# Gate block 1 in seven-product steps, its weight sums begun earlier, in a float32 residual block on one core

## The chip, the cores and the metric

One core of one Trainium2 chip runs the whole program. A core has TensorE (matrix products into the eight PSUM banks), VectorE, ScalarE and GpSimd (elementwise work) and queues that issue DMAs; SP, ScalarE and GpSimd issue them here. The profile calls the engines PE (PEld for its weight loads), DVE, ACT, POOL and SP. The metric is device time in microseconds, a median over runs.

## The reference

One layer of a residual block on x of 512 positions by 1024 channels, all in float32 (cut to what matters):

```python
h = rms_norm(x, norm_mix_g)
cb, cc, cin, q, k, v, f_logit, g_logit = jnp.split(h @ w_in, ...)
u = causal_dwconv(cc * cin, conv_mix_w)
y_conv = (cb * u) @ w_out_conv
o = forgetting_attention(q, k, v, log_sigmoid(f_logit + b_f))   # 8 heads of 64
y_attn = o @ w_out_attn
g_conv, g_attn = jnp.split(sigmoid(g_logit + b_gate), 2, axis=-1)   # 2 x 1024 channels
x = x + (g_conv * y_conv + g_attn * y_attn) @ w_o
a, b = jnp.split(causal_dwconv(rms_norm(x, norm_ffn_g) @ w_up, conv_ffn_w), 2, axis=-1)
x = x + (silu(a) * b) @ w_down
return rms_norm(x, norm_f_g)
```

## The kernel before

Activations lie transposed, channels on the 128 partitions and the 512 positions along the free dimension; 1024 channels are KB = 8 blocks. Every float32 operand is used as a high and a low part (`wh`, `wl` of a weight, `xgh`, `xgl` of the normalised input), and a product is three matmuls: high by high, low weight by high x, high weight by low x. One such matmul has 128 weights columns and 256 positions.

Weights stream in chunks in the order of the list `stream`. A chunk is loaded by an SP DMA into a ring of buffers (`load`; the ring `raw` holds four chunks), then split: ScalarE copies the rounded high part (`wh_...`, L275) and VectorE subtracts (`wl_...`, L279). High and low parts have two buffers each, so a split waits until TensorE is done with the chunk before the last.

The stages follow each other on TensorE: values (`pa`, `pb`); queries and keys of two head pairs (`q0`, `k0`, `q1`, `k1`, functions `proj` and `evac_qk`); the attention, 37 steps in which scores, transposes and weighted values alternate with the halves of the other projections; then a loop over the eight output blocks j that makes the gates, the two branch outputs (`mix` chunk, banks `yc` and `ya`), and the merged block; then `w_o`, the up projection and the down projection in two phases.

In the gate loop a block can be made in two ways. Plain: two `proj` calls, 2 x 8 x 3 x 2 = 96 matmuls. Or in seven-product steps (`seven`, `gate_pair`): the 2 x 2 blocks of weights and of x are combined in sums, so that seven products replace eight, 84 matmuls for a block. Such a step (a pair of quarters q of the 1024 inputs) reads two chunks: P, plain weight blocks, from the input, and F, sums of weight blocks. The sums are made in DRAM by DMAs ahead of time (`make_forms`): for a group of two steps six DMAs, three copies issued on SP and three accumulating ones (`add`) issued on GpSimd's queue, each of which needs the one before to have landed. `slot()` marks a place in the program; a DMA set for slot s is issued when the count reaches s. GROUPS gives for each kind of step the steps per group, the slots between the six DMAs, and the slots between groups. Sums of x are made once: `x_scale` and `x_sums` in the attention, then `x_split(q)` cuts quarter q into `xth` (ScalarE) and `xtl` (VectorE). Small deferred pieces like these wait in the list `later`; `run_later` issues them with splits that have room, `flush` all that is left, `flush_only` those with a given tag.

Blocks j < GJ are plain; block 0 is made at the end of the attention (chunks `in20`, `in28`, in `gp`). A merged block needs the gates times rb1 (VectorE, L891), a sigmoid (ScalarE, with a load of its table), the products with `yc` and `ya` (VectorE, L987, L988), their sum on GpSimd (L989), and its parts `mh` (ScalarE) and `ml` (VectorE). The order of DMAs and matmuls is that of the program; a scheduler sets the order of the rest on each engine.

Of the kernel before, what the change touches and what calls it, by code (L numbers as in the profile page):

```python
# [16 lines left out]
KB = D // P  # L17
# [34 lines left out]
    + (((1, 6),), ((1, 7), (1, 8)), ((1, 9), (1, 10))),  # L52
)

GJ = 2
GATES = tuple(((j, q), (j, q + 1)) for j in range(GJ, KB) for q in (0, 2))

PLAIN = [(m, k) for m in (6, 7) for k in range(*PHASES[1])]
# [5 lines left out]
DOUBLES = GATES + UPD[0] + STEPS[0] + UPD[1] + STEPS[1]  # L64
NU = [len(GATES), len(GATES + UPD[0] + STEPS[0])]
ND = [NU[i] + len(UPD[i]) for i in range(2)]
GROUPS = {"gate": (2, 4, 1), "up0": (2, 4, 1), "up1": (2, 4, 1), 0: (2, (0, 3, 14, 18, 22, 26), 1), 1: (2, 3, 1)}


@with_exitstack  # L70
def block_kernel(ctx, tc, xT, vecs, wv, win, wmix, wo, wup, wst, wdp, outT):
# [3 lines left out]
    nc = tc.nc  # L75
# [6 lines left out]
    def keep(ins):  # L82
        return tc.keep_in_program_order(ins)
# [4 lines left out]
    def ring(*ids):  # L88
        st = [0]

        def f(name):
            st[0] += 1
            return bank(ids[(st[0] - 1) % len(ids)], name)

        return f
# [45 lines left out]
    ff0 = len(stream)  # L141
# [22 lines left out]
        return st  # L164

    def tag_of(k):
        return "raw" if stream[k][0][0] != "F" else "rf" if k >= ff0 else "rg"

    def load(upto):
        for k in range(len(raws), min(upto, len(stream) - 1) + 1):  # L170
            nm, src, ncol = stream[k]
            tag = tag_of(k)
            if held[tag] == NRAW[tag] or tag not in pools:
                return
            held[tag] += 1
            raw = pools[tag].tile([P, D], F32, tag=tag, name=f"raw_{nm}", bufs=NRAW[tag])
            if k == 0:

                keep(nc.scalar.dma_start(raw[:, VB:ncol], src[:, VB:]))
                keep(nc.sync.dma_start(raw[:, :VB], src[:, :VB]))  # L180
            else:
                keep(nc.sync.dma_start(raw[:, :ncol], src if tag == "raw" else made[src]))
            raws.append(raw[:, :ncol])


# [2 lines left out]
    made, todo_bg = {}, []  # L188

    def make_forms(n0, n1, key, start=0):  # L190

        size, step, shift = GROUPS[key]
        if not start:
            make_forms.slot = 0
        cuts = [n0]
        for n in range(n0 + 1, n1 + 1):
            if n == n1 or n - cuts[-1] == size or len(DOUBLES[n]) != len(DOUBLES[cuts[-1]]):
                cuts.append(n)
        for g, (a, b) in enumerate(zip(cuts, cuts[1:])):
            m = len(DOUBLES[a]) * P  # L200
            f = dr.tile([P, b - a, 4 * m], F32, tag=f"f{a}", name=f"f{a}")
            w = wst[a:b].rearrange("n p c -> p n c")
            x0, x1, x2 = w[:, :, 3 * m : 5 * m], w[:, :, 5 * m : 7 * m], w[:, :, 7 * m : 8 * m]
            for n in range(a, b):
                made[n] = f[:, n - a, :]

            def put(dst, src):
                return lambda: keep(nc.sync.dma_start(dst, src))

            def add(dst, src):  # L210
                return lambda: keep(nc.gpsimd.dma_start(dst, src, accum_op=ALU.add))  # L211

            f0, f1, f2 = f[:, :, : 2 * m], f[:, :, 2 * m : 3 * m], f[:, :, 3 * m :]
            ops = (put(f0, x0), add(f0, x1), put(f1, f[:, :, :m]), add(f1, x1[:, :, m:]), put(f2, f1), add(f2, x2))
            todo_bg.extend((start + (step * k if isinstance(step, int) else step[k]) + shift * g, op) for k, op in enumerate(ops))
        todo_bg.sort(key=lambda w: w[0])

    def slot():

# [33 lines left out]
    def split(hl=None):  # L253

        k = len(parts)
        if k == len(stream):
            return
        nm, _, ncol = stream[k]
        load(k + (LOOK if len(raws) > KB else AHEAD))
        if hl is None:  # L260
            hl = []
            for x in "hl":
                if k == 0:
                    wp.tile([P, PADW[x]], F32, tag=f"pad{x}", name=f"pad_{x}")
                w0 = VOFF if k < KB else 0
                hl.append(wp.tile([P, D], F32R, tag=f"w{x}", name=f"w{x}_{nm}", bufs=2)[:, w0 : w0 + ncol])
        hi, lo = hl
        raw = raws[k]
        if k == 0:
            for cs in (slice(VB, S + H), slice(0, VB)):  # L270
                keep(nc.vector.tensor_copy(hi[:, cs], raw[:, cs]))
        elif k == 1:
            keep(nc.vector.tensor_copy(hi, raw))
        else:
            ins = nc.scalar.activation(hi, raw, AF.Copy)  # L275
            order["hi"] = ins.ins
            if k < KB:
                keep(ins)
        ins = nc.vector.tensor_sub(lo, raw, hi.bitcast(F32))  # L279
        order["lo"] = ins.ins  # L280
        if k < KB:
            keep(ins)
        held[tag_of(k)] -= 1
        parts.append((hi, lo))
        if any(("e",) in w[2] for w in later):
            run_later(k, {"u": 4.2, "P": 1.6, "F": 1.2}[nm[0]])
            return
        run_later(k, {"u": 1.7, "P": 1.6, "F": 0.75, "i": 3.0, "m": 3.0, "d": 0 if nm == "dp1" else 2.1}.get(nm[0], 3.5))
# [80 lines left out]
    def rstd_sb(pb, name):  # L369
        rb = cp.tile([P, S], F32, tag="rb", name=f"rb_{name}")  # L370
        nc.scalar.activation(rb, pb, AF.Copy)
        return rb
# [130 lines left out]
    def proj(idx, name, evac, bank):  # L503
        st = {}

        def half(i):
            if i == 0:
                st["w"] = chunk(f"in{idx}")
                st["p"] = bank(f"p_{name}")
            wh, wl = st["w"]  # L510
            for kb in range(4 * i, 4 * i + 4):
                ks = slice(kb * P, (kb + 1) * P)
                mm3(st["p"], wh[:, ks], wl[:, ks], xgh[:, kb, :], xgl[:, kb, :], kb == 0, kb == KB - 1)
            if i == 1:

                while len(parts) < chunk.n + 2:
                    split()
                with after_split():
                    evac(st["p"])

        return [lambda: half(0), lambda: half(1)]
# [151 lines left out]
    def run_all(fs):  # L673
        for f in fs:
            f()

    split()
    split()

# [45 lines left out]
    for t in (2, 3):  # L725
        evac_v(1, t)

    st = []
    f0, f1 = proj(12, "q0", st.append, ring(7))
    f0()  # L730
    rb1 = rstd_sb(rstd_bc(rc1, NT, 6, "n1"), "n1")
    f1()
    pz = bank(4, "pz")
# [3 lines left out]
        ))  # L737
    with after_split():
        forget()
    run_all(proj(16, "k0", st.append, ring(6)))  # L740
    with after_split():
        forget_rows()
        evac_qk(0, True)(st[0])
        evac_qk(0, False)(st[1])
    run_all(proj(13, "q1", evac_qk(1, True), ring(0)))
    run_all(proj(17, "k1", evac_qk(1, False), ring(1)))
    acc, bank_s, bank_t = ring(2, 0, 1), ring(3, 4), ring(5, 6)

    for q in range(4):
# [41 lines left out]
    units = [(pr, e, qb) for pr in range(4) for hf in range(2) for qb in (2 * hf, 2 * hf + 1) for e in range(2)]  # L791
    LT, LA = 3, 5
    n = len(units)
    make_forms(0, len(GATES), "gate")
    for i in range(n + LA):
        slot()
        if i < n:
# [6 lines left out]
        if 0 <= i - LA < n:  # L804
            pr, e, qb = units[i - LA]
            if e == 1 and qb % 2 == 1:
                attend(pr, qb // 2)
    assert not todo_bg
    at.close()

    halves_of = "p (h c) -> p h c"
# [6 lines left out]
    def split_next():  # L818
        if len(parts) == chunk.n and stream[chunk.n][0] not in ("dp1", "dp2"):
            split()  # L820
# [60 lines left out]

    def mt(name):
        mt.n += 1
        return xm[:, (mt.n + 3) % KB, :]

    mt.n = 0

    def evac_gate(idx, dst):
        def f(p):
# [69 lines left out]
    for j in range(KB):  # L959
        gs = []  # L960
        for _ in range(3):
            slot()
        if j == KB - 1:
            assert mt.n == 3 * KB
            x1 = xm
            nc.gpsimd.dma_start(x1[:, :4, :], xT[:, :4, :])
        if j == 0:
            evac_gate(0, gs)(gp[0])
            evac_gate(8, gs)(gp[1])
        elif j < GJ:  # L970
            run_all(proj(20 + j, f"ga{j}", evac_gate(j, gs), acc))
            run_all(proj(28 + j, f"gb{j}", evac_gate(8 + j, gs), acc))
        else:
            if j == GJ:
                acc = ring(3, 4, 2, 7)
            seven(GATES[2 * (j - GJ) : 2 * (j - GJ) + 2], 2 * (j - GJ), {j: (0, 1, 5, 6)}, gate_form, done=gate_pair(j, gs))
        wh, wl = chunk(f"mix{j}")
        yc, ya = acc(f"yc{j}"), acc(f"ya{j}")
        for pp, hh, ll, o in ((yc, ych, ycl, 0), (ya, oth, otl, 4)):
            for k in range(4):  # L980
                ks = slice((o + k) * P, (o + k + 1) * P)
                mm3(pp, wh[:, ks], wl[:, ks], hh[:, k, :], ll[:, k, :], k == 0, k == 3)
        if j >= GJ:
            split_next()
            flush()
        a, b = gs
        nc.vector.tensor_mul(a, a, yc)  # L987
        nc.vector.tensor_mul(b, b, ya)  # L988
        nc.gpsimd.tensor_add(a, a, b)  # L989
        nc.scalar.activation(mh[:, j, :], a, AF.Copy)  # L990
        nc.vector.tensor_sub(ml[:, j, :], a, mh.bitcast(F32)[:, j, :])
# [550 lines left out]
```

## Time and profile before

| what | us |
|---|---|
| median of 3 runs (lowest to highest) | 691.93 (691.58 to 691.97) |
| profiled execution: span, the only time the page gives for it | 690.3 |
| TensorE busy | 682.4 |
| VectorE busy | 556.0 |
| ScalarE busy | 368.5 |
| GpSimd busy | 190.9 |

The span runs from the first to the last instruction of one profiled execution. A timeline row gives the start, the time taken, the engine, the line, the operation, what is written and read, the shapes, how many instructions are merged, and in brackets the idle time of the engine before it and what ended it. The attention ends at about 182 us in this profile, block 0's `mix` matmuls begin at 182.60, block 1's gates at 188.11, and block 2's at 204.43.

### The profile page before, as it was taken

How to read it: one execution, taken by the hardware profiler on the slowest of the kernel's cores; microseconds unless marked ns; L12 is line 12 of the kernel's file. 1: busy time of each engine (PE TensorE's matmuls, PEld its weight loads, DVE VectorE, ACT ScalarE, POOL GpSimd, SP SyncE). 2: the span in 40 equal slices, each digit the busy share in tenths (PEclk: the TensorE clock that was granted, in tenths of full speed). 3: DMA queues.
4: the chain of work that ended last, by engine and by line, in shares of the span. 5: the costliest groups of instructions: out<-in, count | busy, mean ns of one | idle time of the engine just before them, and what ended most of it. 6: DMA issues, size and time to landing. Idle time of an engine off the chain costs nothing.

```text
span 690.3 us, 14714 instructions
## 1 busy us (share of the span) xinstructions
PE 682.4 (99%) x5936; PEld 681.1 (99%) x5936; DVE 556.0 (81%) x861; ACT 368.5 (53%) x581; POOL 190.9 (28%) x203
## 2 busy tenths in 40 slices
PE   9999999999999999999999999999999999999996
PEld 9999999999999999999999999999999999999995
DVE  6677887966578778868879699998786998998894
ACT  5575755555555444446554455546444555445672
POOL 6124946543021201213410144330100314332000
PEclk9999999999999999999999999999999999999998
DMA  8628999562577586788997498889945996776613
GB/s 309 221 62 287 216 239 219 124 138 88 166 168 204 165 263 203 231 311 213 162 309 232 126 241 233 179 240 257 248 150 172 296 265 166 172 186 167 186 31 123
DMA packets 66165, 137.54 MB, mean 199 GB/s; under 512 B 5888, under 2 KB 31760, under 8 KB 65840
## 3 DMA queue, kind: packets, MB, share of 16 engines
q1 hardware_dynamic: 45384, 107.28, 47.0%
q0 software_dynamic: 18896, 26.03, 24.4%
q10 hardware_dynamic: 1816, 3.29, 1.3%
q8 instruction: 46, 0.75, 0.4%
q14 instruction: 23, 0.19, 0.1%
HBM read 132.31 MB, written 47.71 MB: 261 GB/s over the span
## 4 chain that ended last, share of the span: by engine, by line
PE 99%; DVE 0%; DVEq 0%; issue 0%
PE dn L327 29%; PE p_up L309 21%; PE p_in L309 14%; PE p_up L327 6%; PE p_wo L309 6%; PE yc L309 3%; PE ya L309 3%; PE pa L477 2%; PE pb L479 2%; PE p_q L309 2%; PE p_k L309 2%; PE o L658 2%; PE tp L641 1%; PE pdB L309 1%; PE pdA L309 1%; PE s L612 1%
## 5 line engine op out<-in xcount | busy, mean ns | idle before, releaser
L211 POOL DMA_DIRECT2D f<-in_wst_dram x69 | 79.6, 1350 | 26.7 <-DMA f<-f 26.4
L309 PE MATMUL p_up<-x1h,wh_up 128*128 128x256 f32 x416 | 81.1, 276 | 0.0
L309 PE MATMUL p_up<-x1l,wh_up 128*128 128x256 f32 x416 | 81.0, 276 | 0.0
L309 PE MATMUL p_up<-x1h,wl_up 128*128 128x256 f32 x416 | 80.9, 276 | 0.0
L279 DVE TENSOR_TENSOR wl_F<-raw_F,wh_F 128x1024 fp32r<-128x1024 f32 (+1 forms) x43 | 56.1, 1304 | 19.0 <-ACT wh_F L275 18.9
L275 ACT ACTIVATE wh_F<-raw_F 128x1024 fp32r<-128x1024 f32 (+1 forms) x43 | 44.5, 1034 | 39.9 <-PE dn L327 26.4
L309 PEld LDWEIGHTS p_up<-x1h,wh_up 128*128 128x128 f32 x416 | 62.7, 188 | 0.0
L309 PEld LDWEIGHTS p_up<-x1l,wh_up 128*128 128x128 f32 x416 | 62.6, 188 | 0.0
L309 PEld LDWEIGHTS p_up<-x1h,wl_up 128*128 128x128 f32 x416 | 62.6, 188 | 0.0
L309 PE MATMUL p_in<-xgh,wh_in 128*128 128x256 f32 x288 | 56.8, 279 | 0.0
L309 PE MATMUL p_in<-xgh,wl_in 128*128 128x256 f32 x288 | 56.6, 278 | 0.0
L309 PE MATMUL p_in<-xgl,wh_in 128*128 128x256 f32 x288 | 56.5, 278 | 0.0
L1235 POOL TENSOR_TENSOR ge<-fu,fu 128x512 f32<-128x512 f32 x11 | 21.6, 1968 | 124.1 <-DVE fu L570 94.0
L279 DVE TENSOR_TENSOR wl_P<-raw_P,wh_P 128x768 fp32r<-128x768 f32 (+1 forms) x43 | 42.2, 981 | 14.5 <-ACT wh_P L275 8.7
L275 ACT ACTIVATE wh_P<-raw_P 128x768 fp32r<-128x768 f32 (+1 forms) x43 | 35.3, 820 | 33.5 <-PE dn L327 23.1
L327 PE MATMUL dn<-gl,wh_F 128*128 128x256 f32 x216 | 51.0, 276 | 0.0
L327 PE MATMUL dn<-gh,wh_F 128*128 128x256 f32 x216 | 51.0, 276 | 0.0
L279 DVE TENSOR_TENSOR wl_up<-raw_up,wh_up 128x1024 fp32r<-128x1024 f32 x34 | 45.2, 1328 | 6.3 <-ACT wh_up L275 6.3
L275 ACT ACTIVATE wh_up<-raw_up 128x1024 fp32r<-128x1024 f32 x34 | 35.9, 1055 | 20.7 <-PE p_up L309 10.1
L309 PEld LDWEIGHTS p_in<-xgh,wh_in 128*128 128x128 f32 x288 | 44.7, 188 | 0.7
L309 PEld LDWEIGHTS p_in<-xgl,wh_in 128*128 128x128 f32 x288 | 43.7, 188 | 0.0
L309 PEld LDWEIGHTS p_in<-xgh,wl_in 128*128 128x128 f32 x288 | 43.6, 188 | 0.0
(343 smaller groups left out, 2212.1 us busy)
## 6 DMA issues: line engine op xcount, KB each, us to landing
raw_F<-f SPq DMA_DIRECT2D x40, 512.0 KB, 5.5
raw_up<-in_wup_dram SPq DMA_DIRECT2D x34, 512.0 KB, 5.5
raw_P<-in_wst_dram SPq DMA_DIRECT2D x40, 384.0 KB, 5.7
raw_in<-in_win_dram SPq DMA_DIRECT2D x24, 512.0 KB, 3.8
f<-in_wst_dram POOLq DMA_DIRECT2D x41, 256.0 KB, 7.4
f<-in_wst_dram SPq DMA_DIRECT2D x19, 512.0 KB, 7.2
f<-in_wst_dram POOLq DMA_DIRECT2D x19, 512.0 KB, 8.4
f<-f SPq DMA_DIRECT2D x38, 256.0 KB, 6.0
```

What stands on the lines that cost most here:

```text
L211: return lambda: keep(nc.gpsimd.dma_start(dst, src, accum_op=ALU.add))
L275: ins = nc.scalar.activation(hi, raw, AF.Copy)
L279: ins = nc.vector.tensor_sub(lo, raw, hi.bitcast(F32))
L309: keep(nc.tensor.matmul(out[:, cs], w, x[:, cs], start=start and i == 0 and c == 0, stop=stop and i == 2 and c == len(cut) - 1,))
L327: keep(nc.tensor.matmul(out, wl if x == 1 else wh, xl if x == 2 else xh, start=opens and bk not in seen, stop=closes and bk not in left,))
L477: keep(nc.tensor.matmul(pa[t][:, :VW], xt, w[:, VB:], start=start, stop=stop))
L479: keep(nc.tensor.matmul(pb[t], xt, w[:, :VB], start=start and t % 2 == 0, stop=stop and t % 2 == 1))
L612: keep(nc.tensor.matmul(s[:, :nn], QT[pr][:, e, qs], KA[pr][:, e, :nn], start=True, stop=False))
L641: keep(nc.tensor.transpose(tp[:, ks], pt[:, ks], ident))
L658: keep(nc.tensor.matmul(o[:, 2 * P * e + c0 : 2 * P * (e + 1)], w, x[:, kb, c0:], start=e == 0 and kb == 0 and i == 0, stop=e == 1 and kb ...
L1235: keep(nc.gpsimd.tensor_mul(ge, a.rearrange(halves_of, h=2), b.rearrange(halves_of, h=2)))
```

## The change

Block 1's gates are made in seven-product steps as blocks 2 to 7 are (GJ from 2 to 1). There are 14 gate steps instead of 12, in seven groups instead of six. The DMAs of the weight sums begin with the query and key stage, with eight slots set there, and are spread: three slots between the six DMAs of a group and five between groups, before four and one. F0 and F1, which are loaded while the attention's tiles still hold the place of the gates' own ring, go into the ring `raw`. At block 0, quarters 0 and 1 of the x forms are split right after the gates' evacuation, and everything deferred is flushed after the `mix` matmuls. The count of `mt`, which hands out eight places in turn for gate tiles, starts so that it ends where it did.

```diff
-GJ = 2
+GJ = 1
-GROUPS = {"gate": (2, 4, 1), ...
+GROUPS = {"gate": (2, 3, 5), ...
     def tag_of(k):
-        return "raw" if stream[k][0][0] != "F" else "rf" if k >= ff0 else "rg"
+        return "raw" if stream[k][0][0] != "F" or stream[k][0] in ("F0", "F1") else "rf" if k >= ff0 else "rg"
     def make_forms(n0, n1, key, start=0):
-        if not start:
-            make_forms.slot = 0
+        start += make_forms.slot
+    def run_slots(fs):
+        for f in fs:
+            slot()
+            f()
+    make_forms(0, len(GATES), "gate")
     f0, f1 = proj(12, "q0", st.append, ring(7))
+    slot()
     f0()
+    slot()
-    run_all(proj(16, "k0", st.append, ring(6)))
+    run_slots(proj(16, "k0", st.append, ring(6)))
...
-    run_all(proj(13, "q1", evac_qk(1, True), ring(0)))
-    run_all(proj(17, "k1", evac_qk(1, False), ring(1)))
+    run_slots(proj(13, "q1", evac_qk(1, True), ring(0)))
+    run_slots(proj(17, "k1", evac_qk(1, False), ring(1)))
...
-    make_forms(0, len(GATES), "gate")
     for i in range(n + LA):
         slot()
...
     def mt(name):
         mt.n += 1
-        return xm[:, (mt.n + 3) % KB, :]
-    mt.n = 0
+        return xm[:, mt.n % KB, :]
+    mt.n = (2 * GJ - 1) % KB + 4 * KB
...
         if j == 0:
             evac_gate(0, gs)(gp[0])
             evac_gate(8, gs)(gp[1])
+            with after_split():
+                flush_only([("q", 0), ("q", 1)])
...
-        if j >= GJ:
-            split_next()
-            flush()
+        split_next()
+        flush()
```

VectorE at the end of the attention and around block 0's merge, before: `otl` is the last of the attention, the two `xm<-p_in` are block 0's gates, `xtl` the low parts of the x forms, quarter 0 first.

```order
L670 TENSOR_TENSOR otl<-oc_2594,oth 128x256
L891 TENSOR_TENSOR xm<-p_in_2429,rb_n_534 128x512
L891 TENSOR_TENSOR xm<-p_in_2515,rb_n_534 128x512
L987 TENSOR_TENSOR xm<-xm,yc_2628 128x512
L988 TENSOR_TENSOR xm<-xm,ya_2629 128x512
L279 TENSOR_TENSOR wl_in_2741<-raw_in_2410,wh_in_2740 128x1024
L902 TENSOR_TENSOR xtl<-xt,xth 128x1024
L991 TENSOR_TENSOR ml<-xm,mh 128x512
L902 TENSOR_TENSOR xtl<-xt,xth 128x1024
L279 TENSOR_TENSOR wl_mix_2751<-raw_mix_2502,wh_mix_2750 128x1024
L902 TENSOR_TENSOR xtl<-xt,xth 128x1024 x2
```

The same place on VectorE in the changed kernel.

```order
L671 TENSOR_TENSOR otl<-oc_2600,oth 128x256
L898 TENSOR_TENSOR xm<-p_in_2434,rb_n_542 128x512
L898 TENSOR_TENSOR xm<-p_in_2521,rb_n_542 128x512
L909 TENSOR_TENSOR xtl<-xt,xth 128x1024
L995 TENSOR_TENSOR xm<-xm,yc_2639 128x512
L996 TENSOR_TENSOR xm<-xm,ya_2640 128x512
L909 TENSOR_TENSOR xtl<-xt,xth 128x1024 x3
L999 TENSOR_TENSOR ml<-xm,mh 128x512
L280 TENSOR_TENSOR wl_F_2725<-raw_F_2414,wh_F_2724 128x1024
L280 TENSOR_TENSOR wl_P_2757<-raw_P_2507,wh_P_2756 128x768
```

Quarter 0's `xtl` now stands ahead of the products with `yc` and `ya`, the other three right behind them, and the low part of F0 behind those and `ml`.

ScalarE at the same place, before: `xm<-xm,vec` are the two sigmoids, `xth` the high parts of the x forms.

```order
L669 ACTIVATE oth<-oc_2594 128x256
L892 ACT_TABLE_LOAD
L892 ACTIVATE xm<-xm,vec 128x512 x2
L275 ACTIVATE wh_in_2740<-raw_in_2410 128x1024
L901 ACTIVATE xth<-xt 128x1024
L990 ACTIVATE mh<-xm 128x512
L901 ACTIVATE xth<-xt 128x1024
L275 ACTIVATE wh_mix_2750<-raw_mix_2502 128x1024
L901 ACTIVATE xth<-xt 128x1024 x2
```

And in the changed kernel.

```order
L670 ACTIVATE oth<-oc_2600 128x256
L908 ACTIVATE xth<-xt 128x1024
L899 ACT_TABLE_LOAD
L899 ACTIVATE xm<-xm,vec 128x512 x2
L908 ACTIVATE xth<-xt 128x1024 x3
L998 ACTIVATE mh<-xm 128x512
L276 ACTIVATE wh_F_2724<-raw_F_2414 128x1024
L276 ACTIVATE wh_P_2756<-raw_P_2507 128x768
```

Quarter 0's `xth` goes ahead of the table load, the other three behind the sigmoids, and the high part of F0 comes after them and `mh`.

TensorE at the start of block 1 in the changed kernel (before, `p_ga` with `xgh` and `xgl` alone stands there): the first six matmuls, of quarter 0.

```order
L328 MATMUL dn_2702<-xgh,wh_P_2579 128x256
L328 MATMUL dn_2702<-xgl,wh_P_2579 128x256
L328 MATMUL dn_2700<-xgh,wh_P_2579 128x256
L328 MATMUL dn_2700<-xgl,wh_P_2579 128x256
L328 MATMUL dn_2701<-xth,wh_P_2579 128x256
L328 MATMUL dn_2701<-xtl,wh_P_2579 128x256
```

The next six are the same for quarter 1, then six with `wl_P`; then F0, sixteen matmuls with `wh_F` (`xgh`, `xgl`, `xth`, `xtl` of quarters 0 and 1) and eight with `wl_F`. That is the first half of block 1, 42 matmuls, and the second half does the same with P1, F1 and quarters 2 and 3.

GpSimd in the query and key stage, before: `qb` and `a_k` are parts of queries and keys, `pp` the scaled attention weights.

```order
L699 MEMSET fo 32x512
L555 TENSOR_SCALAR qb_113<-t_q_639 64x512 x2
L555 TENSOR_SCALAR a_k_652<-t_k_650 64x512 x2
L536 DMA qb_114<-fr 2x512 x2
L536 DMA kb_116<-fr 2x512 x2
L555 TENSOR_SCALAR qb_114<-t_q_716 64x512 x2
L555 TENSOR_SCALAR a_k_784<-t_k_782 64x512 x2
L625 TENSOR_SCALAR pp_809<-pp_809,m_807 128x128
L625 TENSOR_SCALAR pp_844<-pp_844,m_842 128x128
```

And in the changed kernel, with the adds of weight sums (`f`) between.

```order
L705 MEMSET fo 32x512
L210 DMA f_504<-in_wst_dram 256x1x512
L556 TENSOR_SCALAR qb_113<-t_q_648 64x512 x2
L556 TENSOR_SCALAR a_k_661<-t_k_659 64x512 x2
L537 DMA qb_114<-fr 2x512 x2
L537 DMA kb_116<-fr 2x512 x2
L210 DMA f_505<-in_wst_dram 256x1x512
L556 TENSOR_SCALAR qb_114<-t_q_726 64x512 x2
L556 TENSOR_SCALAR a_k_795<-t_k_793 64x512 x2
L626 TENSOR_SCALAR pp_814<-pp_814,m_812 128x128
L210 DMA f_504<-in_wst_dram 256x1x256
L626 TENSOR_SCALAR pp_849<-pp_849,m_847 128x128
```

Three adds, of groups 0 and 1, come ahead of work that feeds the first scores and transposes. On SP the copy of group 1 stands behind the pair of `kb` DMAs.

More of the change, by code (lines that the diff above doesn't have):

```diff
@@ L66 @@
 ND = [NU[i] + len(UPD[i]) for i in range(2)]
-GROUPS = {"gate": (2, 4, 1), "up0": (2, 4, 1), "up1": (2, 4, 1), 0: (2, (0, 3, 14, 18, 22, 26), 1), 1: (2, 3, 1)}
+GROUPS = {"gate": (2, 3, 5), "up0": (2, 4, 1), "up1": (2, 4, 1), 0: (2, (0, 3, 14, 18, 22, 26), 1), 1: (2, 3, 1)}
 @with_exitstack
@@ L181, in load @@
             else:
-                keep(nc.sync.dma_start(raw[:, :ncol], src if tag == "raw" else made[src]))
+                keep(nc.sync.dma_start(raw[:, :ncol], made[src] if nm[0] == "F" else src))
             raws.append(raw[:, :ncol])
@@ L216, in make_forms @@
         todo_bg.sort(key=lambda w: w[0])
+    make_forms.slot = 0
     def slot():
@@ L807, in block_kernel @@
                 attend(pr, qb // 2)
-    assert not todo_bg
     at.close()
@@ L963, in block_kernel @@
         if j == KB - 1:
-            assert mt.n == 3 * KB
+            assert mt.n % KB == 3
             x1 = xm
```

## The prediction

> **What bounds the kernel now.** I read the page first (span, busy shares, the chain that ended last), then the waits of the weight loads, which stand for TensorE's own waits, then the timeline of each engine around the place of the change.
>
> ```profile
> span 690.3 us, 14714 instructions
> ...
> PE 682.4 (99%) x5936; PEld 681.1 (99%) x5936; DVE 556.0 (81%) x861; ACT 368.5 (53%) x581; POOL 190.9 (28%) x203
> ...
> PE 99%; DVE 0%; DVEq 0%; issue 0%
> ```
> ```profile
> PEld warm L115 <- DVE ones L107: 1.1, 1, 1.1
> PEld dn L327 <- DVE wl_P L279: 0.2, 1, 0.2
> ```
>
> TensorE is the whole chain: apart from the start it waited 0.2 us for another engine in the entire span. So a matmul less is worth its full pace, and every wait put in front of TensorE is paid in full, since nothing later has slack to give back. The span is the only time the page gives for the profiled execution; it lies 1.6 us under the median of the runs (691.93), and I take that rest as unchanged and add every term to 691.93.
>
> **What is removed from TensorE.** Block 1 of the gates runs from the first `p_ga` to the next `yc`; block 2, already in seven-product steps, from its first `dn` to its `yc`.
>
> ```profile
> 188.11 0.39 PE L309 MATMUL p_ga<-xgh,wh_in 128*128 128x256 f32 x2
> ...
> 198.99 0.39 PE L309 MATMUL yc<-ych,wh_mix 128*128 128x256 f32 x2
> ...
> 204.43 0.28 PE L327 MATMUL dn<-xgh,wh_P 128*128 128x256 f32 x1
> ...
> 213.95 0.39 PE L309 MATMUL yc<-ych,wh_mix 128*128 128x256 f32 x2
> ```
>
> 10.88 us for 96 matmuls and 9.52 us for 84: both 113.3 ns each. Block 1 changes from the first to the second, so TensorE has 12 matmuls or **1.36 us** less to do. That alone gives 691.93 - 1.36 = 690.6.
>
> **What block 1 now waits for.** The plain block needed only `xgh` and `xgl`, which have been there since the start. The new one needs the summed x forms `xth` and `xtl` of quarters 0 and 1 in its very first weight chunk, and its F chunk soon after. With block 1 beginning at 188.11 as before, the matmuls in the order shown above need: `xth`, `xtl` of quarter 0 as the 5th and 6th, at 188.6; those of quarter 1 as the 11th and 12th, at 188.11 + 10 x 0.1133 = 189.24 and 189.36; `wh_F` as the 19th, at 190.15; `wl_F` as the 35th, at 191.96; and the first half ends after 42, at 192.87. Now when can these be ready? ScalarE and VectorE before:
>
> ```profile
> 184.59 0.42 ACT L669 ACTIVATE oth<-oc 128x256 fp32r<-128x256 f32 x1 [0.49 <-DVE oc L667]
> 186.26 1.28 ACT L892 ACT_TABLE_LOAD   x1 [1.25 <-DVE xm L891]
> 187.56 1.34 ACT L892 ACTIVATE xm<-xm,vec 128x512 f32<-128x512 f32 x2
> 188.80 1.05 ACT L275 ACTIVATE wh_in<-raw_in 128x1024 fp32r<-128x1024 f32 x1
> 189.75 1.05 ACT L901 ACTIVATE xth<-xt 128x1024 fp32r<-128x1024 f32 x1
> 191.09 0.63 ACT L990 ACTIVATE mh<-xm 128x512 fp32r<-128x512 f32 x1 [0.29 <-POOL xm L989]
> ...
> 194.71 1.99 ACT L901 ACTIVATE xth<-xt 128x1024 fp32r<-128x1024 f32 x2
> ...
> 204.68 1.07 ACT L275 ACTIVATE wh_F<-raw_F 128x1024 fp32r<-128x1024 f32 x1 [1.81 <-PE ya L309]
> ```
> ```profile
> 185.04 0.43 DVE L670 TENSOR_TENSOR otl<-oc,oth 128x256 fp32r<-128x256 f32 x1 [0.48 <-ACT oth L669]
> 185.50 1.29 DVE L891 TENSOR_TENSOR xm<-p_in,rb_n 128x512 f32<-128x512 f32 x2
> ...
> 188.93 0.69 DVE L988 TENSOR_TENSOR xm<-xm,ya 128x512 f32<-128x512 f32 x1
> 189.88 2.25 DVE L279 TENSOR_TENSOR wl_in<-raw_in,wh_in 128x1024 fp32r<-128x1024 f32 x1 [0.27 <-ACT wh_in L275]
> 192.06 1.21 DVE L902 TENSOR_TENSOR xtl<-xt,xth 128x1024 fp32r<-128x1024 f32 x1
> 193.19 0.68 DVE L991 TENSOR_TENSOR ml<-xm,mh 128x512 fp32r<-128x512 f32 x1
> ...
> 196.07 2.35 DVE L902 TENSOR_TENSOR xtl<-xt,xth 128x1024 fp32r<-128x1024 f32 x2
> ```
>
> Each row gives start and duration. ScalarE's new order is one `xth`, the table load, the two sigmoids, three `xth`, `mh`, `wh_F`. The first `xth` writes where the attention's tiles lay, so it follows their last reader, `otl`, at 185.47: done at 186.5, and VectorE has its `xtl` after the two gate products at 188.0, in time for 188.6. Then the table load (1.28) to 187.8, two sigmoids (1.34) to 189.15, and quarter 1's `xth` (1.05, neighbours overlap by 0.1) to 190.1: already 0.9 us late.
>
> VectorE's `xtl` of quarter 1 stands behind the product with `ya`, which waits for the second sigmoid: 189.2 to 189.9. That product releases GpSimd's sum of the two branches, and here the rows show a collision:
>
> ```profile
> 189.76 1.29 POOL L989 TENSOR_TENSOR xm<-xm 128x512 f32<-128x512 f32 x1 [17.88 <-DVE xm L988]
> ...
> 205.47 1.30 POOL L989 TENSOR_TENSOR xm<-xm 128x512 f32<-128x512 f32 x1 [12.34 <-DVE xm L988]
> ```
> ```profile
> 205.77 2.07 DVE L279 TENSOR_TENSOR wl_F<-raw_F,wh_F 128x1024 fp32r<-128x1024 f32 x1 [0.39 <-ACT wh_F L275]
> ```
>
> A 128x1024 difference of two SBUF tiles takes 1.21 us alone, but 2.25 and 2.07 when it begins 0.12 and 0.30 us after this GpSimd sum; in both cases it ends 1.07 us after the sum does. In the new order GpSimd runs 190.0 to 191.3 and quarter 1's `xtl` begins at 190.15, so it ends at 192.4 instead of 191.35.
>
> Now add up on TensorE. Quarter 1's `xtl` at 192.4 instead of 189.36: **3.0 us** of waiting. The other seven matmuls of the chunk end at 193.2, but `wh_F` isn't there: after quarter 1's `xth` (190.1) ScalarE has two more (to 192.0), `mh` (to 192.6) and `wh_F` (1.07, to 193.55). **0.4 us** more. Sixteen matmuls later, at 195.4, `wl_F` is wanted: VectorE does two more `xtl` (2.35, to 194.7), `ml` (0.68, to 195.3) and `wl_F` (1.21, to 196.4). **1.0 us** more. The first half then ends at 196.4 + 8 x 0.1133 = 197.3 instead of 192.87, 4.45 us late. Behind that the splits of chunk 1 need no more than 1.2 us each and are ready in time: `wl_P` at 197.3 for 198.7, `wh_F` at 197.5 for 199.4.
>
> So the sum is -1.36 + 4.45 = +3.1, and 691.93 + 3.1 = **695.0 us**. The lower end of this case is without the collision: `xtl` at 191.35, `wh_F` still at 193.55 (a ScalarE chain of durations alone: 3.4 us late), `wl_F` at 195.4 just in time: 3.45 - 1.36 = +2.1, 694.0. I take the upper one, since the nearest rows, the same sum followed within 0.3 us by the same kind of difference, all show the long form. The own range of this case is 693.7 to 695.5.
>
> [...]
>
> **The rest.** The split of `in21` and `in29` goes, two P and two F splits come; they run beside TensorE once the first half is over. The merge of the partial products copies what block 2 did, with no wait. The weight sums begin eight slots earlier. On GpSimd an add for group 1 now stands ahead of the q1 and k1 work, and waits for its copy to land:
>
> ```profile
> 48.37 1.40 SPq L536 DMA_DIRECT2D kb<-fr  x2
> ```
> ```profile
> 54.03 1.78 POOL L555 TENSOR_SCALAR qb<-t_q 64x512 fp32r<-64x512 f32 x2 [1.06 <-DVE t_q L543]
> ...
> 60.38 1.11 POOL L625 TENSOR_SCALAR pp<-pp,m 128x128 f32<-128x128 f32 x2
> ```
> ```profile
> 65.04 0.27 PE L641 MATMUL tp<-ident,pp 128*128 128x128 f32 x1
> ```
> ```profile
> f<-in_wst_dram SPq DMA_DIRECT2D x19, 512.0 KB, 7.2
> ...
> f<-in_wst_dram POOLq DMA_DIRECT2D x19, 512.0 KB, 8.4
> ```
>
> The copy issues after the `kb` pair, at 49.8, and lands 7.2 later at 57.0. The add (1.1) and two pairs like `qb` (1.8 each) put the first `pp` at 61.7 instead of 60.4; its transpose comes at 65.04. So 2.9 us of cover stays and I cost it at nothing; gone, the late part is paid on TensorE. On SP a weight load can now stand behind an add's landing (8.4); the ring holds four chunks of 48 x 0.113 = 5.4 us, so three in hand cover 16 us. Also nothing; and a gain can't come from there, as TensorE waits for neither before. The bound for both together is 0 to +3.
>
> **Rivals.**
> No wait (690.6): quarter 1's forms are ready by 189.36, because I misplace the order in time. For it: ScalarE stood idle 1.25 us ahead of the table load. Against: from `otl` to that `xtl` the durations in the rows add up to 4.6 us on ScalarE alone, with 3.9 us to do it in. This is the case that ends on the other side; it decides below 1.36 us of waiting.
> A short wait (691.1 to 693.3): `mh` and `wh_F` earlier than I think, and no collision. Against: `wh_F` depends on no guess but the queue's order.
> The early adds hold up the attention (696 to 698): that needs a copy that lands 2.9 us later than the median of 7.2, and then the same again in later groups.
> The clock drops in the pause. After the last matmul the granted clock fell:
>
> ```profile
> 682.91 0.61 PE L363 MATMUL pb_n<-ident,rc_n 128*128 128x128 f32 x4
> ```
> ```profile
> 686.00:691.00 5.00, 0.00 (x0) 0.00 (x0) 0.10 (x1) 0.00 (x0) 0.00 (x0) 0.53 0.43 150
> ```
>
> A mean of 0.53 over 5 us means a drop to 0.5 at about 686.3, 2.8 us after the end at 683.5. TensorE's longest pause here is 190.2 to 192.4, 2.2 us. What a drop would cost, the start shows:
>
> ```profile
> 1.05 4.21 PE L115 MATMUL warm<-ones 128*128 128x128 f32 x18 [1.05 <-DVE ones L107]
> ...
> 6.37 0.63 PE L479 MATMUL pb<-wh_v,xgh 128*128 128x256 f32 x2
> ...
> 7.41 0.40 PE L477 MATMUL pa<-wl_v,xgh 128*128 128x264 f32 x2
> ```
>
> The first matmul stands at 1.05, and a pair still takes 0.63 us at 6.4 and 0.40 from 7.4 on: about 6 us until full pace. At half pace for that long I estimate 3 us more: 698. [...]
>
> **Chances.** My forecast (693.7 to 695.5) 0.70; no wait 0.12; short wait 0.07; clock 0.06; early adds 0.05. 0.2% is 1.4 us, about what a measurement of this kernel can tell from no change. No wait ends at -1.36, on that border, and I split it: faster 0.05, same 0.07. With the short wait same is 0.14; the rest, 0.81, is slower. The range 690.5 to 695.8 takes in the forecast, the short wait and nearly all of no wait, and leaves out the two above.
>
> **What the profile after would show.** Right: TensorE waiting for VectorE's `xtl` (L909) some 2 to 3 us, then for ScalarE's `wh_F` and VectorE's `wl_F` near 1 us together, all between 189 and 197; an `xtl` of about 2.2 us; 5924 matmuls; block 1 taking 14.0 us from first `dn` to `yc`. Wrong: TensorE's waits as short as before and block 1 at 9.5 us; or new waits before 182, which would mean the adds.

## The result, and the profile after

The changed kernel takes 695.31 us (694.98 to 696.69), the kernel before 691.93 beside it: ratio 1.0053, interval 1.0041 to 1.0064. It is slower by 3.4 us; forecast were 695.0 and slower.

First the page (span, busy times, the chain that ended last) and TensorE's waits, as they answer to those of before:

```profile
span 693.8 us, 14716 instructions
...
PE 683.0 (98%) x5924; PEld 680.3 (98%) x5924; DVE 558.7 (81%) x868; ACT 370.1 (53%) x584; POOL 193.6 (28%) x206
...
PE 62%; DVE 0%; DVEq 0%; issue 0%
```
```profile
PEld dn L328 <- DVE xtl L909: 2.1, 1, 2.1
PEld dn L328 <- DVE wl_F L280: 1.2, 2, 1.0
...
PEld dn L328 <- ACT xth L908: 1.0, 1, 1.0
PEld dn L328 <- ACT wh_P L276: 0.4, 1, 0.4
PEld dn L328 <- DVE wl_P L280: 0.2, 1, 0.2
PEld dn L328 <- ACT wh_F L276: 0.2, 1, 0.2
```

The busy shares have hardly moved, and twelve matmuls are gone. What is new stands in the waits: after the start, 5.1 us of TensorE's time behind VectorE and ScalarE, where there were 0.2. The chain shows TensorE for only 62% because the profile follows it back no further than 258.2 us, to the last of these waits (`wh_P`, in block 5); from there to the end it is TensorE nearly throughout. The timelines of ScalarE, VectorE and GpSimd around block 1 (start, duration, engine, line, operation, output and inputs, idle time ahead and its releaser):

```profile
185.46 1.06 ACT L908 ACTIVATE xth<-xt 128x1024 fp32r<-128x1024 f32 x1 [0.49 <-DVE otl L671]
186.54 1.28 ACT L899 ACT_TABLE_LOAD   x1
187.84 1.34 ACT L899 ACTIVATE xm<-xm,vec 128x512 f32<-128x512 f32 x2
189.08 2.94 ACT L908 ACTIVATE xth<-xt 128x1024 fp32r<-128x1024 f32 x3
191.92 0.62 ACT L998 ACTIVATE mh<-xm 128x512 fp32r<-128x512 f32 x1
192.44 1.04 ACT L276 ACTIVATE wh_F<-raw_F 128x1024 fp32r<-128x1024 f32 x1
```
```profile
189.21 0.69 DVE L996 TENSOR_TENSOR xm<-xm,ya 128x512 f32<-128x512 f32 x1
190.15 4.52 DVE L909 TENSOR_TENSOR xtl<-xt,xth 128x1024 fp32r<-128x1024 f32 x3 [0.26 <-ACT xth L908]
194.59 0.68 DVE L999 TENSOR_TENSOR ml<-xm,mh 128x512 fp32r<-128x512 f32 x1
195.20 1.21 DVE L280 TENSOR_TENSOR wl_F<-raw_F,wh_F 128x1024 fp32r<-128x1024 f32 x1
```
```profile
190.04 1.27 POOL L997 TENSOR_TENSOR xm<-xm 128x512 f32<-128x512 f32 x1 [14.81 <-DVE xm L996]
```

And TensorE: the first matmul of block 1, the four that come late, and the first after the block:

```profile
188.12 0.28 PE L328 MATMUL dn<-xgh,wh_P 128*128 128x256 f32 x1
...
190.17 0.38 PE L328 MATMUL dn<-xth,wh_P 128*128 128x256 f32 x1 [0.76 <-ACT xth L908]
192.45 0.38 PE L328 MATMUL dn<-xtl,wh_P 128*128 128x256 f32 x1 [1.90 <-DVE xtl L909]
...
193.54 0.38 PE L328 MATMUL dn<-xgh,wh_F 128*128 128x256 f32 x1
...
196.46 0.38 PE L328 MATMUL dn<-xgh,wl_F 128*128 128x256 f32 x1 [0.82 <-DVE wl_F L280]
...
202.35 0.39 PE L310 MATMUL yc<-ych,wh_mix 128*128 128x256 f32 x2
```

Block 1 takes 202.35 - 188.12 = 14.23 us where the plain one took 10.88. By distance from the matmul ahead, less the pace of 0.113, the four stand 0.92, 2.17, 0.16 and 0.98 us late, and after three of them the second matmul is another 0.11 late. The rest of the span's 3.5 us is read from the same starts in both traces: block 2 takes 9.88 instead of 9.52 and block 5 10.06 instead of 9.52; the other gate blocks keep 9.52. And one term goes the other way. VectorE's last work is the last scaling of the output:

```profile
683.56 2.55 DVE L1417 TENSOR_TENSOR xm<-xm,pb_n 128x256 f32<-128x256 f32 x5 [0.80 <-PE pb_n L363]
```
```profile
687.82 2.55 DVE L1425 TENSOR_TENSOR xm<-xm,pb_n 128x256 f32<-128x256 f32 x5 [0.80 <-PE pb_n L364]
```

The first row is of before, the second of after: 4.26 us later, which is 3.35 + 0.36 + 0.54 within 0.01. But the span ends only 3.5 later, so what lies behind that row is 0.76 us shorter; the last section shows what differs there.

### The profile page after: what moved, and what is told of

Its sections match the earlier page's. It is cut to its first block, busy times and chain, and to the rows that moved or that the text cites. A ratio compares the mean times of both kernels' runs of the same rounds, so it can differ in the third digit from the quotient of the medians.

```text
span 693.8 us, 14716 instructions
## 1 busy us (share of the span) xinstructions
PE 683.0 (98%) x5924; PEld 680.3 (98%) x5924; DVE 558.7 (81%) x868; ACT 370.1 (53%) x584; POOL 193.6 (28%) x206
## 4 chain that ended last, share of the span: by engine, by line
PE 62%; DVE 0%; DVEq 0%; issue 0%
PE dn L328 24%; PE p_up L310 20%; PE p_wo L310 6%; PE p_up L328 6%; PE ya L310 1%; PE yc L310 1%; PE pdB L310 1%; PE pdA L310 1%; PE pc_n L345 0%; DVE xm L1425 0%; PE pb_n L364 0%; PE warm_to L1431 0%; DVE wl_P L280 0%; DVEq L1545 0%; DVE fu L571 0%; PE pdB L1444 0%
## 5 line engine op out<-in xcount | busy, mean ns | idle before, releaser
L280 DVE TENSOR_TENSOR wl_F<-raw_F,wh_F 128x1024 fp32r<-128x1024 f32 (+1 forms) x45 | 57.7, 1283 | 18.5 <-ACT wh_F L276 18.3
L276 ACT ACTIVATE wh_F<-raw_F 128x1024 fp32r<-128x1024 f32 (+1 forms) x45 | 46.5, 1034 | 40.6 <-PE dn L328 28.0
L276 ACT ACTIVATE wh_P<-raw_P 128x768 fp32r<-128x768 f32 (+1 forms) x45 | 37.0, 821 | 39.5 <-PE dn L328 25.3
```

## The experiments

The theory: ScalarE and VectorE come to block 1's x forms and first F weights too late, because block 0's table load, sigmoids, products, sum and parts stand ahead of them, and the sum on GpSimd holds up an `xtl`. The rival in the first runs: the weight sums, begun earlier on SP's and GpSimd's queues, cost the time. Times are medians; each ratio is to runs of the kernel before in the same batch on the same chip, whose medians lay between 691.58 and 692.04. Block durations come from the profiled execution of each.

| run | us | ratio to before | block 1, us |
|---|---|---|---|
| before | 691.93 | 1 | 10.88 |
| after | 695.31 | 1.0053 (1.0041 to 1.0064) | 14.23 |
| a: sums as before | 695.59 | 1.0063 (1.0049 to 1.0077) | 14.33 |
| b: block 1 plain, rest as changed | 697.77 | 1.0087 (1.0073 to 1.0101) | 15.25 |
| b3: as b, without the other ring | 696.10 | 1.0058 (1.0047 to 1.0070) | 15.42 |
| b2: earlier sums alone | 691.69 | 0.9996 (0.9987 to 1.0004) | 10.88 |
| f: without the other ring | 695.02 | 1.0045 (1.0033 to 1.0057) | 14.15 |
| c: sum on VectorE, end of block 0 late | 693.86 | 1.0028 (1.0017 to 1.0039) | 12.50 |
| c2: sum on VectorE, where it was | 694.53 | 1.0038 (1.0026 to 1.0051) | 14.64 |
| d: forms ahead of the sigmoids | 696.88 | 1.0073 (1.0060 to 1.0085) | 15.11 |
| e: F weights ahead too | 690.66 | 0.9984 (0.9975 to 0.9992) | 10.39 |
| e2: a third xth ahead of wh_F | 690.37 | 0.9977 (0.9968 to 0.9987) | 9.52 |
| e3: and block 2's load sooner | 689.77 | 0.9971 (0.9961 to 0.9982) | 9.52 |

**Undoing the sums (a).**

```diff
-GROUPS = {"gate": (2, 3, 5), ...
+GROUPS = {"gate": (2, 4, 1), ...
-    make_forms(0, len(GATES), "gate")      # ahead of q0; and the eight slot() there
+    make_forms(0, len(GATES), "gate")      # ahead of the attention's loop
```

> Block 1 in seven-product steps, but the weight sums issued from the attention on, every four slots, as before the change. The theory (block 1 stands waiting for its own x forms and its first F weights, behind ScalarE's and VectorE's queues; the sums cost nothing): 695.3 us, within 0.5, with the same waits for xtl (about 2.1 us), wh_F and wl_F between 189 and 197. The rival (the earlier sums on GpSimd and SyncE's queue cost the time): 690.6 to 693.5, without them the 1.36 us of fewer matmuls shows.

695.59, and the first two waits of block 1 are the same:

```profile
PEld dn L328 <- DVE xtl L907: 2.1, 1, 2.1
...
PEld dn L328 <- ACT xth L906: 1.0, 1, 1.0
PEld tp L642 <- POOL qb L556: 0.7, 1, 0.7
```

The rival falls. The wait for `wl_F` is missing here: the clock was halved from 193.1 on (last section), so that TensorE came to `wl_F` only at 197.01, after it was ready, and block 1 is just 0.1 us longer than in after. The third line stands in the attention: a transpose waits once for GpSimd's copy `qb`. Neither after nor the kernel before, which has the old schedule with one group less, shows this wait.

**Block 1 plain, all else as changed (b), and b without the other ring (b3).**

```diff
-GJ = 1
+GJ = 2
```

> Block 1 as eight plain products again, all else as changed (earlier sums, the other ring for the first two F chunks, x forms split sooner). The theory: 691.9 us, within 0.5, and TensorE waits for nothing but the start. The rival (the earlier sums cost the time): 693 to 696.5, with waits of TensorE left somewhere.

> Block 1 plain, earlier sums, x forms split sooner, but the F ring as before. If the three x forms ahead of the plain block's second weight split are the cost (2.9 us of waiting and 1.5 us of halved clock in the run with the new ring), they stay and only the 1.2 us of later waits for F weights may go: 696.4 to 697.9 us. If the ring were the cost: 692.

697.77, the slowest of all, where the theory as I held it said 691.9. TensorE stood here, in block 1's second product, for VectorE (b's TensorE, then VectorE):

```profile
195.99 0.80 PE L310 MATMUL p_gb<-xgh,wl_in 128*128 128x256 f32 x2 [2.44 <-DVE wl_in L280]
```
```profile
189.66 4.54 DVE L909 TENSOR_TENSOR xtl<-xt,xth 128x1024 fp32r<-128x1024 f32 x3 [0.27 <-ACT xth L908]
194.12 0.68 DVE L999 TENSOR_TENSOR ml<-xm,mh 128x512 fp32r<-128x512 f32 x1
194.72 1.21 DVE L280 TENSOR_TENSOR wl_in<-raw_in,wh_in 128x1024 fp32r<-128x1024 f32 x1
```

Three `xtl` and `ml` now stand ahead of the weight split that the plain block needs. So splitting the x forms sooner is no free half of the change: ahead of a plain block it is nearly as dear as the late forms are for the new one (block 1 is 4.4 us longer, 2.6 of it this wait and some 1.6 a halved clock). Before, the plain block's `wl_in` came first of all, and two of the forms after `wl_mix`. b3, at 696.10 just under its forecast range, keeps the 2.6 us and loses only the later waits, 0.9 us for `wh_F` and 0.3 for `wl_F` in block 3: the ring is not the cause, and costs something only once all is late.

**The earlier sums alone (b2), and the ring undone in the changed kernel (f).** b2 is b3 with the forms split where they were before; f is a single line of `tag_of`.

```diff
-            with after_split():                      # b2
-                flush_only([("q", 0), ("q", 1)])
-        split_next()
-        flush()
+        if j >= GJ:
+            split_next()
+            flush()
```

> Block 1 plain, x forms split where they were before the change, the F ring as before: of the change only the earlier and spread weight sums are left. The theory (the sums cost nothing): 691.9 us, within 0.5, no wait of TensorE above 0.3 us after the start. The rival (part of the 5.9 us of the run with plain block 1 comes from the sums): 693 to 696.

> Of the change only the other ring for the first two F chunks is undone: they are loaded into the ring that opens behind the attention. The theory (the queues' order is the whole cost; raw_F, issued near 185.6 and landing in some 5 us, is there before ScalarE comes to it at 192.4): 695.3 us, within 0.5. The rival (the load is too late without the other ring): wh_F later, 696 us or more.

691.69 and 695.02, both as the theory said. In b2 TensorE waits for nothing above 0.2 us after the start. Sums and ring cost nothing.

**Taking block 0's end out of the way (c), and the collision alone (c2).**

```diff
+        def tail(j=j, a=a, b=b):
+            (nc.gpsimd if j else nc.vector).tensor_add(a, a, b)
+            ...                                      # mh, ml
+        if j: tail()
+        else:
+            split()
+            with after_split(): tail()               # c
```
```diff
-        nc.gpsimd.tensor_add(a, a, b)
+        (nc.gpsimd if j else nc.vector).tensor_add(a, a, b)   # c2, where it stood
```

> Only block 0's end is changed: the sum of its two branches goes from GpSimd to VectorE, and it, mh and ml are issued behind the first F chunk's split. The theory: quarter 1's xtl takes 1.2 us instead of 2.2 and ends at 191.4; wh_F ends at 192.96, wl_F at 194.9; on TensorE 2.0 + 0.85 + 0.1 = 2.95 us of waiting instead of 4.3, so 695.3 - 1.35 = 693.9 us (693.4 to 694.2). [...]

> One instruction is changed: block 0's sum of its two branches runs on VectorE, where it was, not on GpSimd. The theory (the sum on GpSimd holds up quarter 1's xtl by 1.07 us, and the operations themselves cost the rest): VectorE spends 0.6 more on the sum, xtl ends at 191.7 instead of 192.4, wh_F still at 193.5, wl_F at 195.8 instead of 196.4; 3.85 us of waiting instead of 4.25, 694.8 us (694.2 to 695.0). The rival (no collision, the operation is as slow whatever GpSimd does): xtl ends at 193.0, 4.9 us of waiting, 696 us.

VectorE in c, then in c2:

```profile
190.01 3.50 DVE L909 TENSOR_TENSOR xtl<-xt,xth 128x1024 fp32r<-128x1024 f32 x3 [0.26 <-ACT xth L908]
```
```profile
189.35 0.69 DVE L997 TENSOR_TENSOR xm<-xm 128x512 f32<-128x512 f32 x1
189.96 3.48 DVE L909 TENSOR_TENSOR xtl<-xt,xth 128x1024 fp32r<-128x1024 f32 x3
```

Three `xtl` take 3.5 us instead of 4.52, in both: the missing 1.0 us is the collision. Block 1 of c takes 12.50, that is 2.98 us over full pace for the 2.95 of waiting worked out. That its median meets the forecast of 693.9 is partly luck: the profiled run took 693.01, with blocks 2 and 5 at 9.5 us again, which the forecast did not count. The four runs from 693.86 to 694.66 show a mean granted clock of 0.994 to 0.996, the other three 0.998 to 0.999, so that a halved stretch in those four is likely, but no profile of them shows it. In c2 the three waits are 0.92, 1.53 and 0.80, 3.25 for 3.85; its median agrees with the forecast for a wrong reason, since its profile has a stretch of halved clock that the forecast did not have (below).

**Only the forms in time (d).** Both products of the gates first, then the forms of quarters 0 and 1, then the sigmoids.

```diff
-            evac_gate(0, gs)(gp[0])
-            evac_gate(8, gs)(gp[1])
+            ...                                      # the two tensor_mul
             with after_split():
                 flush_only([("q", 0), ("q", 1)])
+            ...                                      # the two sigmoids, behind the last xth
```

> Only the order is changed: both forms of quarters 0 and 1 come ahead of the table load and block 0's two sigmoids. The theory (three queues are late one behind the other): xtl of quarter 1 is there at 189.1 and TensorE no longer waits for it, but wh_F, behind the sigmoids, two more xth and mh, ends at 193.75 instead of being there at 190.15 (3.6 us), and wl_F at 196.2 instead of 195.6 (0.65 us): 4.25 us instead of 4.3, so 695.2 us (694.7 to 695.5). The rival (the longest wait that the profile names, 2.1 us for xtl and 1.0 for xth, is the cost): without them about 692.2 us.

The wait that the profile of after names first is gone, and the kernel is slower still. TensorE, and windows of TensorE's row (the column behind the engines is the granted clock):

```profile
193.90 0.39 PE L328 MATMUL dn<-xgh,wh_F 128*128 128x256 f32 x1 [3.59 <-ACT wh_F L276]
```
```profile
190.00:194.00 4.00, 0.41 (x4) 0.21 (x2) 3.74 (x4) 3.73 (x6) 3.04 (x3) 1.00 0.05 4
194.00:196.00 2.00, 2.00 (x11) 2.00 (x12) 2.00 (x3) 0.58 (x1) 0.28 (x1) 0.57 0.95 99
196.00:198.00 2.00, 2.00 (x12) 2.00 (x12) 1.06 (x2) 0.58 (x1) 0.00 (x0) 0.58 1.02 137
198.00:200.00 2.00, 2.00 (x19) 2.00 (x18) 1.23 (x1) 0.50 (x2) 0.00 (x0) 1.00 1.07 195
```

`wh_F` is 3.76 us late for 3.6 worked out: the two late things were one behind the other, and taking away the first gains nothing. About 1.0 of the miss of 1.7 us is the clock: after the pause it is halved for 3.4 us, and a matmul takes some 0.21 us instead of 0.113, which costs 1.6 in place of the 0.65 forecast for `wl_F`. Another 0.6 is block 2, which takes 10.50 us where it took 9.88 in after.

**Everything in time (e, e2, e3).** ScalarE and VectorE first make what block 1 needs.

```diff
+            ...                                      # the two tensor_mul, flush_only q0, q1
+        if j == 0:
+            flush_only([("q", 2)])                   # e2, e3
+            split()                                  # F0
         split_next()
         flush()
+            later.append((k, 0, (), sig))            # k: P1; behind its split
+            later.append((k, 0, (), prod))
+            later.append((k + 2, 0, (), tail))       # e, e2; in e3 free, emitted at block 1's end
-        ... stream[k][0] in ("F0", "F1") else ...
+        ... stream[k][0] == "F0" else ...            # e3
```

> All that block 1 needs first goes ahead of block 0's end. ScalarE: two xth, wh_F, two xth, the next wh_P, and only then table load and sigmoids; VectorE in the same order, with the sum of block 0 on VectorE and mh, ml behind the next splits. The theory (the order of the two queues is the whole cost): quarter 1's xtl ends at 189.1, wh_F at 188.4, wl_F at 190.3, all in time; the next F chunk's wh_F at 194.9 just in time; waits of at most 0.4 us in block 1, so the 1.36 us of fewer matmuls show: 690.8 us (690.4 to 691.4), faster than both. The rival (the seven-product block itself or its merge costs time there): 692.5 or more.

> As the run with everything ahead of block 0's end, but with the third xth ahead of the first wh_F, which can't begin before 188.3 (its buffer is read by the last mix product until then). The theory: ScalarE no longer stands 0.85 us; the next F chunk's wh_F ends 0.85 earlier, at 194.8, and TensorE's last wait in block 1 (0.75 us) goes: 690.66 - 0.75 = 689.9 us (689.6 to 690.4). The rival (the time is noise of that size or another wait takes its place): 690.7.

> As the last run, with two things more. Of the first two F chunks only the first is loaded into the other ring, so that block 2's first P chunk finds a place some 5 us sooner; and block 0's sum, mh and ml are tied to no split. In the last run the wait only moved: block 1 ran its 84 matmuls in 9.52 us, but wh_P of block 2 waited for its load until 198.0, mh and ml stood ahead of block 1's merge, and TensorE stood 0.61 us for wh_F and 0.35 us for wl_F at 205.7 and 208.0. The theory (that merge 0.9 us sooner takes both away): 690.4 - 0.95 = 689.4 us (689.2 to 690.0), span near 688.9. The rival (VectorE and ScalarE have no room left between blocks 0 and 2, and another wait comes): 690.3 or more.

e confirms the theory: faster than both kernels. It left a wait of 0.75 us for the next F chunk's `wh_F`, since the first could not start before 188.33 (its buffer was in use until then) and all behind it was late. e2 mends that, and block 1 has no wait at all; but block 2 then takes 10.77 us, so the gain over e is not shown (the intervals overlap). The wait had moved one block on, to a `wh_P` that waited for its load:

```profile
198.01 0.85 ACT L276 ACTIVATE wh_P<-raw_P 128x768 fp32r<-128x768 f32 x1 [2.38 <-DMA raw_P<-in_wst_dram]
```

e3 brings that load forward. ScalarE, then VectorE, then TensorE's first matmul of block 1 and of what follows:

```profile
184.91 2.96 ACT L908 ACTIVATE xth<-xt 128x1024 fp32r<-128x1024 f32 x3 [0.49 <-DVE otl L671]
187.77 1.06 ACT L276 ACTIVATE wh_F<-raw_F 128x1024 fp32r<-128x1024 f32 x1
...
191.82 1.34 ACT L1002 ACTIVATE xm<-xm,vec 128x512 f32<-128x512 f32 x2
```
```profile
186.12 3.49 DVE L909 TENSOR_TENSOR xtl<-xt,xth 128x1024 fp32r<-128x1024 f32 x3
189.52 1.22 DVE L280 TENSOR_TENSOR wl_F<-raw_F,wh_F 128x1024 fp32r<-128x1024 f32 x1
```
```profile
187.56 0.28 PE L328 MATMUL dn<-xgh,wh_P 128*128 128x256 f32 x1
...
197.08 0.39 PE L310 MATMUL yc<-ych,wh_mix 128*128 128x256 f32 x2
```

Blocks 1 to 7 all run at full pace, and the kernel takes 689.77 us, 0.29% less than before (0.18% to 0.39%): the 1.36 us of matmuls and the 0.76 of the shorter end make 2.1, of which the medians show 1.9. The 0.76 are no merit of the order: after has them too.

## Why the prediction was right, point by point

- **Twelve matmuls, 1.36 us:** right; e2 and e3 show block 1 at 9.52 us instead of 10.88.
- **The late forms:** quarter 1's `xtl` was wanted at 189.36, forecast for 192.4 and used at 192.45.
- **The collision:** right in place and size. Three `xtl` in a row took 4.52 us, and 3.50 in c, where the sum was elsewhere. The first of the three began 0.11 us after the sum (190.15 and 190.04), took 2.25 us and ended 1.08 us after it; one alone takes 1.21. By what the sum holds it up, no run shows.
- **`wh_F` and `wl_F` behind them:** forecast for 193.55 and 196.4, used at 193.54 and 196.46. d shows that this was no detail: with the forms in time the wait for `wh_F` grows to 3.76 us.
- **The sum of waits, 4.45 us:** block 1 shows 4.71. Not counted were the 0.11 us that the second matmul loses after a restart, three times, and some slower pace.
- **The sums and SP, costed at nothing:** right (b2, 0.9996); that rival is out. **No wait** and **short wait** are out too.
- **Nothing behind block 1:** wrong. Blocks 2 and 5 lose 0.36 and 0.54 us. And the end of the program is 0.76 shorter, which I had not seen either. The forecast of +3.1 against +3.4 measured is as near as it is by luck, because these two nearly cancel: 3.35 + 0.90 - 0.76 = 3.49.
- **The clock drops in the pause:** not in the profile of after (1.00 in every window around block 1), but the reason that I gave for it, a pause of only 2.2 us where the clock of before fell 2.8 us after the last matmul, does not hold: a, with the same pauses, has the drop. That after escaped it is luck; the last section has the numbers.
- **The x forms split sooner:** the prediction gave this part no price of its own, and the forecast for b took it to be free. b and b3 show 2.6 us of waiting from it where block 1 is plain.

## What to carry to other kernels

On a queue that works in order, put first what the engine that bounds the kernel wants first, and write down for each operand when it is wanted and when its queue comes to it; the first wait that a profile names may hide a second as long right behind it, which only appears when the first is gone. A change that saves work at a seam between two stages needs its operands made before the seam; here the same twelve matmuls fewer cost 3.4 us in one order of the queues and gained 1.9 in another (both with the 0.76 us that the program's end is shorter). When the order is mended, look one block further on: the wait moves.

## What the runs showed that was not expected

**Short pauses can halve the clock.** Read in slices of 0.1 us, the profiles of a, b, b3, c2 and d each have one stretch at 0.5, of 3.41 us, beginning at 193.1, 195.8, 196.6, 192.9 and 194.3. The longest pause ahead was 2.2, 2.6, 2.6, 1.5 and 3.8 us; in c2 three pauses together, 0.92, 1.53 and 0.80:

```profile
190.00:192.00 2.00, 0.77 (x6) 0.77 (x7) 2.00 (x3) 2.00 (x4) 0.00 (x0) 1.00 1.02 149
192.00:194.00 2.00, 1.36 (x8) 1.16 (x7) 2.00 (x4) 1.64 (x2) 0.00 (x0) 0.74 1.12 205
194.00:196.00 2.00, 2.00 (x11) 2.00 (x11) 2.00 (x3) 0.00 (x0) 0.00 (x0) 0.50 0.12 23
```

After and f, with pauses of 0.92 and 2.17, have no such stretch; a, with the same two, has one. At 0.21 us a matmul instead of 0.113, 3.41 us of it cost some 1.6, less where TensorE would have waited anyway, as in a. In four of the five the longest pause was only 1.5 to 2.6 us; in c2 TensorE was without work for about 2.4 of the 3.41 us ahead of the drop, by its matmuls' starts.

One count separates the profiles. Counted in steps of 3.413 us (the slices give the five stretches 3.412 to 3.414) from the moment at which a profile's clock first reached 1.00, each halved stretch is exactly one step, the 56th in a, c2 and d and the 57th in b and b3. A full step begins 30 matmuls. The table has the emptiest step of each of eight profiles, up to the end of the gates; in the other five no step begins fewer than 21.

| run | step ahead, us | matmuls begun | next step |
|---|---|---|---|
| d | 190.87 to 194.28 | 3 | halved |
| a | 189.65 to 193.07 | 4 | halved |
| b3 | 193.15 to 196.57 | 6 | halved |
| b | 192.37 to 195.78 | 7 | halved |
| c2 | 189.53 to 192.94 | 8 | halved |
| f | 187.82 to 191.23 | 13 | full clock |
| c | 187.67 to 191.09 | 13 | full clock |
| after | 190.96 to 194.37 | 14 | full clock |

So in these profiles it is the work within a step that counts, not the length of one pause: steps that began 3 to 8 matmuls of 30 had a halved one behind them, steps that began 13 or more had none. In a both pauses fall almost wholly into one step; in after the line between two steps, at 190.96, cuts the longer pause. Where that line falls differs from one profile to the next; how often after meets the bad case stays open.

**The collision works both ways.** Block 5 of after lost its 0.54 us where, for the first time, VectorE was ahead of GpSimd by 0.04 us (VectorE, GpSimd, TensorE):

```profile
254.38 1.23 DVE L280 TENSOR_TENSOR wl_F<-raw_F,wh_F 128x1024 fp32r<-128x1024 f32 x1
```
```profile
254.42 2.33 POOL L997 TENSOR_TENSOR xm<-xm 128x512 f32<-128x512 f32 x1 [10.92 <-DVE xm L996]
```
```profile
258.20 0.38 PE L328 MATMUL dn<-xgh,wh_P 128*128 128x256 f32 x1 [0.25 <-ACT wh_P L276]
```

The sum then takes 2.33 us instead of 1.29; `mh`, which waits for it, is late, and `wh_P` behind `mh` on ScalarE. The same pair cost TensorE nothing in before, where GpSimd was first by 0.30 us (250.35 and 250.65): there the sum took 1.29 us and `wl_F` 2.07.

**The end of the program.** In all nine profiles with the new block 1 the time from VectorE's last row to the span's end is about 0.76 us shorter than in the four with the plain one (before, b, b2 and b3). VectorE's work and the issues of the output's DMAs have the same times. SP's wait for the last of those DMAs differs (before, then after: us in total, times, longest):

```profile
SPq L1537 <- DMA out_dram<-xm: 2.3, 1, 2.3
```
```profile
SPq L1545 <- DMA out_dram<-xm: 1.5, 3, 0.7
```

The traces show two differences that add up to it. The last DMA has landed, by SP's waits, about 0.45 us sooner. In all four profiles with the plain block an 8 KB packet of the queue that the page calls instruction (q14) runs for about 0.7 us among the output's packets, and in none of the nine others. And SP waits for its queues in a fixed order at some 0.06 us each: with the plain block the last DMA is on a queue early in that order, and seven waits come behind it, with the new one two, 0.3 us less. That the packet is what delays the landing fits all thirteen profiles, but no run changes it alone; why it moves with the kernel was not found.
